# The FFN of a hybrid decoder block by 2x2 blocks in seven products

## The chip, the cores and the metric

The kernel runs on one core of a Trainium2 chip. A time is device microseconds of one execution; the kernel before takes 2752.7 us, the median of three runs (2752.18 to 2753.68).

## The reference

One decoder layer for 512 tokens of width 2048, in fp32: two attention branches, merged by sigmoid gates, and a SwiGLU FFN of width 5632. Only the FFN changes:

```python
    h2 = _rms(x, g_norm2) * (1 + sc2) + sh2
    gate, up = jnp.split(h2 @ w_ffn_in, 2, axis=-1)
    x = x + gt2 * ((jax.nn.silu(gate) * up) @ w_ffn_out)
```

`w_ffn_in` is 2048 x 11264, `w_ffn_out` 5632 x 2048; `sh2`, `sc2` and `gt2` are rows computed from the conditioning vector.

## The kernel before

An fp32 product is made of three matmuls. Each operand is kept as a high part (rounded to the matrix engine's fp32r) and a low part (the rest), and `mm3` sums high x low, high x high and low x high in PSUM. Activations lie with channels on the 128 partitions and tokens along the row (128x512). Weights are the standing operand, 128x128 at a time, and 512 tokens stream past: one output tile is 128 channels x 512 tokens.

The program is a list of steps. A step that needs weights gets a piece of 128x1024, cut from a load of 128x2048 that SP issues (`load`, four buffers). ScalarE copies the piece to `whi`, and VectorE subtracts to get `wlo` (three buffers each), before the step in front of it runs. VectorE, ScalarE and TensorE instructions are put in order by a scheduler where `Ordered` is off; with it on they keep program order.

The FFN's width is cut into 11 groups of four gate tiles and four up tiles. `last_a` and `last_b` make the last tile of the output projection in two token halves, so that the second norm of one half (`last_sum`, `last_row`, `norm2_half`) runs beside products. Group 0 runs k-tile by k-tile into eight PSUM banks (`ff0_first`, `ff0_second`, `ff0`), so each k-tile's norm (`norm_tile`) stands just ahead of its matmuls. Then `ff_in` makes each further group, 8 tiles x 16 k-tiles x 3 = 384 matmuls; `swiglu` evacuates a pair to `act`; and `ffn_out` makes the down projection of the group before, 16 tiles x 4 k-tiles x 3 = 192 matmuls, and VectorE adds each tile, times `gt2`, to the residual `x1`, which stays in SBUF. In the last group each finished tile is stored, 14 from POOL and 2 from SP.

Tiles of 128x512 come from one pool of 68. PSUM has eight banks under the names mm (3), s (2), t (2) and y (1). An instruction issued through `Ordered` has line 82 in every row; loads have line 173.

Of the kernel before, what the change touches and what calls it, by code (L numbers as in the profile page):

```python
# [1279 lines left out]
```

## Time and profile before

| | |
|---|---|
| median of three runs | 2752.7 us |
| span of the profiled execution | 2750.7 us |
| TensorE busy | 2710.9 us |
| VectorE busy | 1401.7 us |
| ScalarE busy | 838.7 us |
| mean DMA rate | 145 GB/s |

The profiled execution is one of the program's executions; its span runs from the first to the last instruction. Matmuls are pipelined, so their listed durations overlap. The time per matmul is the distance between starts.

### The profile page before, as it was taken

The page shows a single profiled execution, that of the slowest core. Times are in us where ns is not written, and L with a number is a line of the kernel's source. Part 1 is how long each engine was busy: PE and PEld are TensorE (multiplying, and loading weights), DVE is VectorE, ACT ScalarE, POOL GpSimd, SP SyncE. Part 2 cuts the span into 40 slices and gives each one's busy share as a digit, 9 for nine tenths or more (in the row PEclk, how much of TensorE's full clock was granted, in tenths as well). Part 3 has the DMA queues.
Part 4 walks back from the last instruction along what each step waited for, and adds up shares of the span by engine and source line. Part 5 has one row for each costly group of instructions (what it writes and reads, how often), then busy time and mean ns, then how long its engine had stood idle before and what let it go on. Part 6 is the DMA issues. An engine that isn't in the chain of part 4 may idle for free.

```text
span 2750.7 us, 30791 instructions
## 1 busy us (share of the span) xinstructions
PE 2710.9 (99%) x12760; PEld 2265.5 (82%) x12760; DVE 1401.7 (51%) x1870; ACT 838.7 (30%) x1145; POOL 39.3 (1%) x85
## 2 busy tenths in 40 slices
PE   5999999999999999999999999999999999999999
PEld 4788888888998888888888888888888888888887
DVE  8966766657887755433543424242424333333333
ACT  4334656533333322222322222222221222222221
POOL 0000000001001000000000000000000000000001
PEclk9999999999999999999999999999999999999999
DMA  9855444346666773332222222222222232232222
GB/s 345 291 189 172 161 137 136 134 158 245 245 232 255 287 297 130 134 122 93 99 101 92 97 102 92 95 105 92 93 106 92 93 107 92 92 107 92 92 105 79
DMA packets 69892, 398.04 MB, mean 145 GB/s; under 512 B 7861, under 2 KB 8117, under 8 KB 27769
## 3 DMA queue, kind: packets, MB, share of 16 engines
q1 hardware_dynamic: 62496, 381.45, 38.7%
q10 hardware_dynamic: 6056, 10.70, 1.0%
q0 software_dynamic: 1200, 3.93, 0.4%
q8 instruction: 100, 1.64, 0.2%
q14 instruction: 40, 0.32, 0.0%
HBM read 381.37 MB, written 14.68 MB: 144 GB/s over the span
## 4 chain that ended last, share of the span: by engine, by line
PE 96%; DVE 2%; DMA 1%; ACT 0%; issue 0%; SPq 0%; ACTq 0%; DVEq 0%
PE ps_mm L82 64%; PE ps_s L82 20%; PE ps_t L82 10%; PE ps_y L82 2%; DVE raw L266 1%; DVE wlo L82 0%; DMA raw<-in_w_ada_dram 0%; DMA xt<-in_xT_dram 0%; DMA gpark<-sg 0%; DVE hl L82 0%; DVE xt L82 0%; DMA consts<-in_consts_dram 0%; ACT whi L82 0%; DVE diag L82 0%; SPq L173 0%
## 5 line engine op out<-in xcount | busy, mean ns | idle before, releaser
L82 ACT CAST whi<-raw 128x1024 fp32r<-128x1024 f32 (+1 forms) x474 | 495.8, 1048 | 1479.9 <-PE ps_mm L82 812.9
L82 DVE TENSOR_TENSOR wlo<-raw,whi 128x1024 fp32r<-128x1024 f32 (+1 forms) x474 | 577.5, 1219 | 692.4 <-ACT whi L82 682.4
L82 PE MATMUL ps_mm<-h2l,whi 128*128 128x512 f32 (+1 forms) x1014 | 393.5, 388 | 0.0
L82 PE MATMUL ps_mm<-h2h,whi 128*128 128x512 f32 (+1 forms) x1014 | 393.2, 388 | 0.0
L82 PE MATMUL ps_mm<-h2h,wlo 128*128 128x512 f32 (+1 forms) x1014 | 393.2, 388 | 0.0
L82 PE MATMUL ps_mm<-hl,whi 128*128 128x512 f32 x832 | 327.5, 394 | 0.0
L82 PE MATMUL ps_mm<-hh,whi 128*128 128x512 f32 x832 | 325.4, 391 | 0.0
L82 PE MATMUL ps_mm<-hh,wlo 128*128 128x512 f32 x832 | 325.4, 391 | 0.0
L82 PE MATMUL ps_s<-acth,whi 128*128 128x512 f32 x704 | 273.9, 389 | 0.0
L82 PE MATMUL ps_s<-acth,wlo 128*128 128x512 f32 x704 | 273.9, 389 | 0.0
L82 PE MATMUL ps_s<-actl,whi 128*128 128x512 f32 x704 | 273.8, 389 | 0.0
L82 DVE SCALAR_TENSOR_TENSOR xr<-ps_s,ada_gt,xr 128x512 f32<-128x512 f32 x176 | 132.1, 751 | 230.9 <-PE ps_s L82 230.9
L266 DVE CUSTOM_DVE_ANT_0 raw<-raw,cb,cols 128x2048 f32<-128x2048 f32 x96 | 224.7, 2346 | 2.1 <-DMA raw<-in_w_ada_dram 2.1
L82 PEld LDWEIGHTS ps_mm<-h2l,whi 128*128 128x128 f32 x1014 | 190.4, 188 | 39.0
L82 PEld LDWEIGHTS ps_mm<-h2h,whi 128*128 128x128 f32 x1014 | 190.4, 188 | 39.0
L82 PEld LDWEIGHTS ps_mm<-h2h,wlo 128*128 128x128 f32 x1014 | 190.4, 188 | 39.0
L82 PEld LDWEIGHTS ps_mm<-hh,wlo 128*128 128x128 f32 x832 | 156.4, 188 | 32.4
L82 PEld LDWEIGHTS ps_mm<-hh,whi 128*128 128x128 f32 x832 | 156.7, 188 | 30.7
L82 PEld LDWEIGHTS ps_mm<-hl,whi 128*128 128x128 f32 x832 | 156.8, 188 | 30.5
L82 PEld LDWEIGHTS ps_s<-actl,whi 128*128 128x128 f32 x704 | 132.2, 188 | 27.6 <-DVE actl L82 0.3
L82 PEld LDWEIGHTS ps_s<-acth,wlo 128*128 128x128 f32 x704 | 132.2, 188 | 27.4
L82 PEld LDWEIGHTS ps_s<-acth,whi 128*128 128x128 f32 x704 | 132.2, 188 | 27.3
(283 smaller groups left out, 3671.6 us busy)
## 6 DMA issues: line engine op xcount, KB each, us to landing
raw<-in_w_ff_dram SPq DMA_DIRECT2D x132, 1024.0 KB, 4.7
raw<-in_w_ada_dram SPq DMA_DIRECT2D x96, 1024.0 KB, 5.2
raw<-in_w_gate_dram SPq DMA_DIRECT2D x27, 1024.0 KB, 5.0
raw<-in_w_sb_dram SPq DMA_DIRECT2D x24, 1024.0 KB, 4.9
raw<-in_w_out_dram SPq DMA_DIRECT2D x16, 1024.0 KB, 4.8
raw<-in_w_gate_dram SPq DMA_DIRECT2D x24, 512.0 KB, 4.5
raw<-in_w_lat_dram SPq DMA_DIRECT2D x8, 1024.0 KB, 8.2
gpark<-sg ACTq DMA_DIRECT2D x32, 256.0 KB, 5.2
```

Source lines behind the costliest of these rows:

```text
L82: ins = f(*a, **kw)
L266: tc.keep_in_program_order(nc.vector.tensor_tensor_reduce(raw, raw, cb, 1.0, col(C_B + 16 * ADA[name] + j), ALU.mult, ALU.add, dst))
```

## The change

The FFN's three matrices are cut into 2x2 blocks: tokens in halves of 256, the summed dimension in halves, the output columns in halves. Seven block products (P1, P5, P7, P3, P6, P2, P4, in this order) and sums of blocks give what eight products gave. Some products have a sum of activation blocks (x12, x34 and so on) on one side and a difference of weight blocks on the other.

- The roles are exchanged: a 128x128 block of activations stands and 512 weight columns stream past, so an output tile has 128 tokens x 512 channels. Gated activations are turned back on TensorE (`act_back1`, `act_back2`, 16 transposes a group).
- Weight blocks are 128x1024 in a pool of ten (`rp2`), loaded six pieces ahead. `piece_make` makes the difference of two raw blocks in place on VectorE where a product has one, then `whi` and `wlo`, two pieces ahead.
- Gate and up of all 11 groups come first, 7 products x 4 pieces x 12 = 336 matmuls a group. The activations' parts and sums are stored to DRAM (`apark`, 14 stores a group, from POOL). The down projection follows in five chunks of groups (`CH`), two column halves each, with 7 x 2 x 12 = 168 matmuls a group; the parts come back by loads from SP, and bank sums are added in `acc`.
- The second norm of all k-tiles is done by `first_norms`, before P1 of group 0, and `second_norms`, before the last piece of P1, which also makes the sums. The residual `x1` is written over by it and waits in DRAM (`xpark`, 17 stores from POOL). `out_tiles` turns the final sums back (64 transposes), loads the residual and stores the result.

```diff
+        ep_cm.__exit__(None, None, None)
+        rp_cm.__exit__(None, None, None)
+        st["rp2"] = ctx.enter_context(tc.tile_pool(name="rp2", bufs=10, reuse_waits="tile"))
+        ffn_begin()
         vec.on = act.on = pe.on = True
         last_mm(0, range(8, 16))
         last_evac(0)
...
+    def norm2(k, th):
         c = half_cols(th)
-        if th == 0:
-            h2.append((t2("h2h", F32R), t2("h2l", F32R)))
-        hi, lo = h2[k]
         gs, sh = ada["gs2"][:, k:k + 1], ada["sh2"][:, k:k + 1]
-        t = t2("nt")
-        vec.scalar_tensor_tensor(t[:, 0:256], x1[k][:, c], gs, st["rstd2"][:, c], ALU.mult, ALU.mult)
-        act.activation(hi[:, c], t[:, 0:256], AF.Identity, bias=sh)
-        vec.scalar_tensor_tensor(lo[:, c], t[:, 0:256], sh, hi[:, c].bitcast(F32), ALU.add, ALU.subtract)
+        t = x1[k][:, c]
+        vec.scalar_tensor_tensor(t, t, gs, st["rstd2"][:, c], ALU.mult, ALU.mult)
...
+    def sums(a, b, put):
+        lo, hi = slice(0, 256), slice(256, 512)
+        s12, s34 = t2("s12"), t2("s34")
+        vec.tensor_tensor(s12[:, lo], a[:, hi], b[:, hi], ALU.add)
+        vec.tensor_tensor(s12[:, hi], s12[:, lo], a[:, lo], ALU.subtract)
+        put(1, split_t(s12, "x12"))
+        vec.tensor_tensor(s34[:, lo], a[:, lo], a[:, hi], ALU.subtract)
+        vec.tensor_tensor(s34[:, hi], b[:, lo], s12[:, hi], ALU.subtract)
+        put(3, split_t(s34, "x34"))
...
+        sums(x1[j], x1[j + 8], put)
...
+    PROD = {
+        "P1": ((1, 1), "11", None), "P5": (1, "12", "11"), "P7": (3, "22", "12"), "P3": (4, "22", None),
+        "P6": (2, "22", "11"), "P2": ((1, 2), "21", None), "P4": ((2, 2), "21", "22"),
+    }
...
+    def piece_make(stage, g, prod, j):
+        _, x, y = PROD[prod]
+        key = (stage, g, x, j)
+        if y:
+            kd = (stage, g, INTO[prod], j)
+            vec.tensor_tensor(raws[kd], raws[key], raws[stage, g, y, j], ALU.subtract)
+            key = kd
+        r = raws[key]
+        hi = wp.tile([P, 1024], F32R, tag="whi", name=nm("whi"), bufs=3)
+        lo = wp.tile([P, 1024], F32R, tag="wlo", name=nm("wlo"), bufs=3)
+        v4 = lambda t: t.rearrange("p (k m c) -> p k m c", k=2, m=4)
+        act.copy(v4(hi), kmc(key, r))
+        vec.tensor_tensor(v4(lo), kmc(key, r), v4(hi).bitcast(F32), ALU.subtract)
+        for b in LAST.get(prod, ()):
+            del raws[stage, g, b, j]
+        return hi, lo
...
+    def ahead_to(i, n_make, n_load):
+        while cur["load"] < min(i + n_load + 1, len(pieces)) or cur["make"] < min(i + n_make + 1, len(pieces)):
+            if cur["load"] <= cur["make"] or cur["load"] < min(i + n_load + 1, len(pieces)):
+                for key in piece_keys(*pieces[cur["load"]]):
+                    raw_load(key)
+                cur["load"] += 1
+            else:
+                made[cur["make"]] = piece_make(*pieces[cur["make"]])
+                cur["make"] += 1
...
+                ahead_to(i, 2, 6)
...
+    def prod_mm(bank, hl, w, kk, first, last):
+        wh, wl = w
+        cs = slice(kk * 512, kk * 512 + 512)
+        xh, xl = hl
+        for t in range(2):
+            mm3(bank[t], (xh[:, t * P:(t + 1) * P], xl[:, t * P:(t + 1) * P]), (wh[:, cs], wl[:, cs]),
+                first, last, skip_group_check=True)
...
+        product("P1", "A", True, False)
+        copy_to("p1", "A")
+        if g > 0:
+            add_do(lambda: act_back2(g - 1))
+        product("P5", "B", True, False)
+        copy_to("z", "B")
+        product("P7", "C", True, False)
+        add_bank("z", "C")
+        product("P3", "B", False, True)
+        product("P6", "D", True, True)
+        def u_of(t):
+            vec.tensor_tensor(G["p1", t], G["p1", t], G["D"][t], ALU.add)
+            G["u", t] = G.pop(("p1", t))
+        both(u_of)
+        both(after_p6)
+        product("P2", "A", False, True)
+        both(after_p2)
+        product("P4", "C", False, True)
+        both(after_p4)
+        add_do(lambda: act_back1(g))
+        groups[g] = G
+    groups = {}
+    apark = [dp.tile([P, 7 * T], F32, name=f"apark_{i}") for i in range(2 * FG)]
...
+        def after_p6(t):
+            u, z = G["u", t], G["z", t]
+            vec.tensor_tensor(z, z, u, ALU.add)
+            c12 = t2("c12")
+            vec.tensor_tensor(c12, u, G["B"][t], ALU.add)
+            G["c12", t] = c12
...
+    def park(i, a, pair):
+        for part, t in enumerate(pair):
+            nc.gpsimd.dma_start(pk(i, a, 2, part), t.bitcast(F32).rearrange("p (a x) -> p a x", a=2))
...
+    def act_back1(g):
+        src = [groups[g].pop(("a1", t)) for t in range(2)]
+        for j in range(2):
+            o = ps(("mm", "y")[j])
+            back(src, j, o)
+            y = t2("y1")
+            act.copy(y, o)
+            park(2 * g + j, 0, split_t(y, "y1"))
+            yraw[g, j] = y
...
+    def act_back2(g):
+        src = [groups[g].pop(("a2", t)) for t in range(2)]
+        for j in range(2):
+            o = ps(("mm", "y")[j])
+            back(src, j, o)
+            y2 = t2("y2")
+            act.copy(y2, o)
+            y1 = yraw.pop((g, j))
+            x = t2("x22", F32R)
+            act.copy(x[:, 0:256], y2[:, 256:512])
+            vec.tensor_tensor(x[:, 256:512], y2[:, 256:512], x[:, 0:256].bitcast(F32), ALU.subtract)
+            nc.gpsimd.dma_start(apark[2 * g + j].rearrange("p (a x) -> p a x", x=T)[:, 2], x.bitcast(F32))
+            lo, hi = slice(0, 256), slice(256, 512)
+            s12, s34 = t2("s12"), t2("s34")
+            vec.tensor_tensor(s12[:, lo], y2[:, lo], y2[:, hi], ALU.add)
+            vec.tensor_tensor(s12[:, hi], s12[:, lo], y1[:, lo], ALU.subtract)
+            park(2 * g + j, 3, split_t(s12, "y12"))
+            vec.tensor_tensor(s34[:, lo], y1[:, lo], y2[:, lo], ALU.subtract)
+            vec.tensor_tensor(s34[:, hi], y1[:, hi], s12[:, hi], ALU.subtract)
+            park(2 * g + j, 5, split_t(s34, "y34"))
...
+    add_do(first_norms)
...
+    at_product(1, lambda: last_sum(1))
+    at_product(2, lambda: last_row(1))
+    def second_norms():
+        for k in range(8):
+            norm2(k + 8, 0)
+            norm2(k, 1)
+            norm2(k + 8, 1)
+            x_sums(k)
...
+    CH = ((0, 1, 2), (3, 4), (5, 6), (7, 8), (9, 10))
...
+                bank = B[BANK[prod]][t]
+                if ci == 0:
+                    a = t2("acc")
+                    act.copy(a, bank)
+                    acc[q, prod, t] = a
+                else:
+                    a = acc[q, prod, t]
+                    vec.tensor_tensor(a, a, bank, ALU.add)
+                if final:
...
+                add_piece(("b", (q, g), prod, 0), use)
+            add_do(lambda prod=prod: evac(prod))
+            if prod == "P1" and ci == q == 0:
+                add_do(lambda: act_back2(FG - 1))
+            if q == 1 and ci + 1 < len(CH):
+                add_do(lambda prod=prod: y_load(ci + 1, prod))
...
+    def out_tiles(q, col_):
+        xr_ = {}
+        for i in range(4):
+            m = 4 * (2 * q + col_) + i
+            xr = t2("xo")
+            sync_dma(xr, xpark[m])
+            xr_[i] = xr
+        for i in range(4):
+            m = 4 * (2 * q + col_) + i
+            o = ps(("mm", "y")[i % 2])
+            for r in range(2):
+                for t in range(2):
+                    pe.transpose(o[:, (2 * r + t) * P:(2 * r + t + 1) * P],
+                                 fin[q, r + 1, col_ + 1, t][:, i * P:(i + 1) * P], ident)
+            xr = xr_[i]
+            vec.scalar_tensor_tensor(xr, o, ada["gt2"][:, m:m + 1], xr, ALU.mult, ALU.add)
+            (nc.gpsimd if m < 14 else nc.sync).dma_start(outT[m * P:(m + 1) * P, :], xr)
```

The order of TensorE's work at the FFN's start. In `h2l` and `h2h` are the parts of one normed k-tile, in `x_...` and `x12...` those of a block and of a sum of two blocks. Before:

```order
L82 MATMUL ps_t_10680<-h2l_10647,whi_10564 128x256
L82 MATMUL ps_t_10680<-h2h_10646,whi_10564 128x256
L82 MATMUL ps_t_10680<-h2h_10646,wlo_10565 128x256
L82 MATMUL ps_t_10681<-h2l_10647,whi_10564 128x256
L82 MATMUL ps_t_10681<-h2h_10646,whi_10564 128x256
L82 MATMUL ps_t_10681<-h2h_10646,wlo_10565 128x256
L82 MATMUL ps_s_10682<-h2l_10647,whi_10564 128x256
L82 MATMUL ps_s_10682<-h2h_10646,whi_10564 128x256
```

Now, from the end of P1 into P5:

```order
L82 MATMUL ps_s_10794<-wlo_10828,x_10776 128x512
L82 MATMUL ps_s_10794<-whi_10827,x_10776 128x512 x2
L82 MATMUL ps_s_10795<-wlo_10828,x_10776 128x512
L82 MATMUL ps_s_10795<-whi_10827,x_10776 128x512 x2
L82 MATMUL ps_t_11103<-wlo_10850,x12h_10881 128x512
L82 MATMUL ps_t_11103<-whi_10849,x12h_10881 128x512
L82 MATMUL ps_t_11103<-whi_10849,x12l_10882 128x512
L82 MATMUL ps_t_11104<-wlo_10850,x12h_10881 128x512
L82 MATMUL ps_t_11104<-whi_10849,x12h_10881 128x512
L82 MATMUL ps_t_11104<-whi_10849,x12l_10882 128x512
```

The matmuls after P1 take the sum x12 where a single normed tile stood.

VectorE at the same place, before: norms of single tiles (`nt`, then `h2l`) beside `wlo`:

```order
L82 TENSOR_TENSOR wlo_10732<-raw_10729,whi_10731 128x1024
L82 SCALAR_TENSOR_TENSOR nt_10750<-xr_9557,ada_gs_160,rstd_10537 128x256
L82 SCALAR_TENSOR_TENSOR h2l_10647<-nt_10750,ada_sh_161,h2h_10646 128x256
L82 SCALAR_TENSOR_TENSOR nt_10754<-xr_9621,ada_gs_160,rstd_10537 128x256
L82 SCALAR_TENSOR_TENSOR nt_10820<-xr_9686,ada_gs_160,rstd_10537 128x512
L82 SCALAR_TENSOR_TENSOR h2l_10653<-nt_10754,ada_sh_161,h2h_10652 128x256
L82 SCALAR_TENSOR_TENSOR h2l_10823<-nt_10820,ada_sh_161,h2h_10822 128x512
```

Now (`xr` is normed in place, `s` holds a sum of blocks, `x12l` and `x34l` its low part):

```order
L82 SCALAR_TENSOR_TENSOR x_10873<-xr_10128,ada_sh_183,x_10873 128x256
L82 SCALAR_TENSOR_TENSOR xr_9732<-xr_9732,ada_gs_182,rstd_10596 128x256
L82 SCALAR_TENSOR_TENSOR xr_10260<-xr_10260,ada_gs_182,rstd_10596 128x256
L82 TENSOR_TENSOR s_1889_10877<-xr_9601,xr_10128 128x256
L82 SCALAR_TENSOR_TENSOR xr_9798<-xr_9798,ada_gs_182,rstd_10596 128x256
L82 TENSOR_TENSOR s_1889_10877<-s_1889_10877,xr_9601 128x256
L82 SCALAR_TENSOR_TENSOR xr_10326<-xr_10326,ada_gs_182,rstd_10596 128x256
L82 SCALAR_TENSOR_TENSOR xr_9864<-xr_9864,ada_gs_182,rstd_10596 128x256
L82 SCALAR_TENSOR_TENSOR xr_10392<-xr_10392,ada_gs_182,rstd_10596 128x256
L82 TENSOR_TENSOR x12l_10882<-s_1889_10877,x12h_10881 128x512
L82 TENSOR_TENSOR s_1890_10878<-xr_9601 128x256
L82 TENSOR_TENSOR s_1890_10878<-xr_10128,s_1889_10877 128x256
```

The norms of many tiles and the first sum stand between two `wlo`.

VectorE inside a group, before: `wlo` and the two operations of `swiglu`:

```order
L82 TENSOR_TENSOR silu_11841<-silu_11841,ps_mm_11786 128x512
L82 TENSOR_TENSOR wlo_11880<-raw_11877,whi_11879 128x1024
L82 TENSOR_TENSOR actl_11845<-silu_11841,acth_11844 128x512
L82 TENSOR_TENSOR wlo_11908<-raw_11877,whi_11907 128x1024
L82 TENSOR_TENSOR wlo_11939<-raw_11936,whi_11938 128x1024
L82 TENSOR_TENSOR wlo_11974<-raw_11936,whi_11973 128x1024
L82 TENSOR_TENSOR silu_11966<-silu_11966,ps_mm_11911 128x512
```

Now, at the end of P6 (`p`, `z`, `c` hold block sums, `raw<-raw,raw` is a difference of weight blocks):

```order
L82 TENSOR_TENSOR wlo_13225<-raw_2329_13149,whi_13224 128x1024
L82 TENSOR_TENSOR p_2278_12888<-p_2278_12888,ps_mm_13175 128x512
L82 TENSOR_TENSOR p_2279_12890<-p_2279_12890,ps_y_13176 128x512
L82 TENSOR_TENSOR z_13024<-z_13024,p_2278_12888 128x512
L82 TENSOR_TENSOR c_2344_13243<-p_2278_12888,ps_t_12957 128x512
L82 TENSOR_TENSOR z_13026<-z_13026,p_2279_12890 128x512
L82 TENSOR_TENSOR c_2345_13246<-p_2279_12890,ps_t_12958 128x512
L82 TENSOR_TENSOR wlo_13249<-raw_2332_13168,whi_13248 128x1024
L82 TENSOR_TENSOR wlo_13265<-raw_2337_13189,whi_13264 128x1024
L82 TENSOR_TENSOR raw_2329_13149<-raw_2329_13149,raw_2275_12869 128x1024
L82 TENSOR_TENSOR wlo_13284<-raw_2326_13130,whi_13283 128x1024
L82 TENSOR_TENSOR raw_2332_13168<-raw_2332_13168,raw_2298_12950 128x1024
```

Six operations of 512 columns now stand between one `wlo` and the next, and differences of weight blocks between those that follow.

## Rows read from the trace of the kernel before

**Rows 1.** page, busy time by engine, and the chain that ended last
```profile
PE 2710.9 (99%) x12760; PEld 2265.5 (82%) x12760; DVE 1401.7 (51%) x1870; ACT 838.7 (30%) x1145; POOL 39.3 (1%) x85
...
PE 96%; DVE 2%; DMA 1%; ACT 0%; issue 0%; SPq 0%; ACTq 0%; DVEq 0%
```

**Rows 2.** busy time by stretch: times, then PE, PEld, DVE, ACT, POOL, clock, DMA share, GB/s
```profile
15.00:20.00 5.00, 0.47 (x3) 0.47 (x3) 4.44 (x8) 4.44 (x8) 0.00 (x0) 1.00 1.04 399
985.00:1010.00 25.00, 25.00 (x112) 20.71 (x111) 14.94 (x18) 7.23 (x10) 0.00 (x0) 1.00 0.92 359
...
1500.00:2000.00 500.00, 500.00 (x2207) 414.20 (x2206) 180.16 (x186) 112.03 (x122) 0.00 (x0) 1.00 0.27 97
2700.00:2751.00 51.00, 46.97 (x207) 38.40 (x205) 20.66 (x24) 6.84 (x7) 7.58 (x14) 1.00 0.22 83
```

**Rows 3.** instructions in order of time, TensorE inside the FFN (start, duration)
```profile
1599.75 0.39 PE L82 MATMUL ps_mm<-h2h,whi 128*128 128x512 f32 x1
...
1602.92 0.39 PE L82 MATMUL ps_mm<-h2l,whi 128*128 128x512 f32 x1
```

**Rows 4.** the same view of TensorE, first FFN products and a gap
```profile
1305.57 0.39 PE L82 MATMUL ps_t<-h2l,whi 128*128 128x256 f32 x1
1305.79 0.28 PE L82 MATMUL ps_t<-h2h,whi 128*128 128x256 f32 x1
...
1308.33 0.61 PE L82 MATMUL ps_y<-ones,sq 128*128 128x1 f32 x4 [1.06 <-DVE sq L82]
```

**Rows 5.** chain of waits over the last 61 us (start, length)
```profile
2703.32 43.67 PE ps_s L82 x192
...
2747.01 0.75 DVE xr L82
```

**Rows 6.** groups by form, TensorE between 400 and 1000 us
```profile
L82 PE MATMUL ps_mm<-whi,hh 128*128 128x256 f32 x256 | 72.4, 283 | 0.0
...
L82 PE MATMUL ps_t<-consts,sa 128*128 128x128 f32 x80 | 11.3, 272 | 0.0
```

**Rows 7.** groups by form between 1450 and 2750 us, all engines
```profile
L82 DVE TENSOR_TENSOR wlo<-raw,whi 128x1024 fp32r<-128x1024 f32 x236 | 289.3, 1226 | 489.3 <-ACT whi L82 481.2
...
L82 ACT CAST whi<-raw 128x1024 fp32r<-128x1024 f32 x236 | 248.4, 1053 | 995.5 <-PE ps_mm L82 496.1 <-PE ps_s L82 336.9 <-PE ps_t L82 162.4
...
L82 DVE SCALAR_TENSOR_TENSOR xr<-ps_s,ada_gt,xr 128x512 f32<-128x512 f32 x162 | 121.6, 751 | 212.8 <-PE ps_s L82 212.8
...
L82 ACT CAST acth<-silu 128x512 fp32r<-128x512 f32 x40 | 24.5, 612 | 0.0
...
L1156 POOL DMA_DIRECT2D out_dram<-xr x14 | 7.6, 542 | 1819.2 <-DVE xr L82 1819.2
```

**Rows 8.** instructions in order of time, VectorE during the attention
```profile
380.56 0.69 DVE L82 CUSTOM_DVE_ANT_0 p<-ps_s,rstd 128x512 f32<-128x512 f32 x1
381.18 0.08 DVE L82 DVE_READ_ACCUMULATOR2_ANT mx<- 128x1 f32 x1
...
383.29 1.23 DVE L82 TENSOR_TENSOR wlo<-raw,whi 128x1024 fp32r<-128x1024 f32 x1
384.44 0.16 DVE L82 RECIPROCAL ri<-sm 128x1 f32<-128x1 f32 x1
...
385.09 0.42 DVE L82 TENSOR_TENSOR ptl<-ps_t,pth 128x256 fp32r<-128x256 f32 x1
```

**Rows 9.** the same view of VectorE, second norm of the first token half
```profile
1303.96 0.48 DVE L82 SCALAR_TENSOR_TENSOR nt<-xr,ada_gs,rstd 128x256 f32<-128x256 f32 x1 [1.26 <-ACT rstd L82]
1305.03 0.49 DVE L82 SCALAR_TENSOR_TENSOR h2l<-nt,ada_sh,h2h 128x256 fp32r<-128x256 f32 x1 [0.58 <-ACT h2h L82]
1305.43 0.48 DVE L82 SCALAR_TENSOR_TENSOR nt<-xr,ada_gs,rstd 128x256 f32<-128x256 f32 x1
```

**Rows 10.** DMA issues: count, KB each, median us from issue to landing
```profile
gpark<-sg ACTq DMA_DIRECT2D x32, 256.0 KB, 5.2
...
out_dram<-xr POOLq DMA_DIRECT2D x14, 256.0 KB, 2.3
```

More of the change, by code (lines that the diff above doesn't have):

```diff
@@ L129 @@
     ypark = [dp.tile([P, T], F32, name=f"ypark_{g}") for g in range(H)]
-    onesw = cp.tile([P, T], F32, name="onesw")
+    xpark = [dp.tile([P, T], F32, name=f"xpark_{g}") for g in range(KD)]
+    onesw = ep.tile([P, T], F32, name="onesw")
     nc.gpsimd.memset(onesw, 1.0)
@@ L175, in load @@
     def load(src, w=2048):
-        raw = wp.tile([P, w], F32, tag="raw", name=nm("raw"), bufs=4)
+        raw = rp.tile([P, w], F32, tag="raw", name=nm("raw"))
         sync_dma(raw, src)
@@ L239, in run_steps @@
             s[0](ahead.pop(i))
-    cb = cp.tile([P, D], F32, name="cb")
+    cb = ep.tile([P, D], F32, name="cb")
     cps = []
@@ new lines, with add_piece, add_do @@
+    ev = []
+    made = {}
+    cur = {"load": 0, "make": 0}
+    pieces = []
+    def add_piece(args, use):
+        pieces.append(args)
+        ev.append((len(pieces) - 1, use))
+    def add_do(fn):
+        ev.append((None, fn))
+    def ahead_to(i, n_make, n_load):
[7 more added lines that the diff above has]
+                cur["make"] += 1
@@ new lines, in tb, with ffn_in_group, product, use @@
+    def tb(*tags):
+        return [ps(t) for t in tags]
+    def ffn_in_group(g, order):
+        G = {}
+        n = KD // 4
+        def product(prod, bank, start, stop):
+            def use(w, j):
+                if j == 0 and start:
+                    G[bank] = tb(*{"A": ("s", "s"), "B": ("t", "t"), "C": ("mm", "mm"), "D": ("mm", "y")}[bank])
+                for kk in range(2):
+                    prod_mm(G[bank], X[PROD[prod][0], 2 * j + kk], w, kk, start and j == 0 and kk == 0,
+                            stop and j == n - 1 and kk == 1)
+            for j in range(n):
+                add_piece(("a", g, prod, j), lambda w, j=j: use(w, j))
+        def both(fn):
+            add_do(lambda: [fn(t) for t in range(2)])
+        def copy_to(name, bank):
+            def fn(t):
+                G[name, t] = t2(name)
+                act.copy(G[name, t], G[bank][t])
+            both(fn)
+        def add_bank(name, bank, out=None):
+            def fn(t):
+                dst = G[name, t] if out is None else t2(out)
+                vec.tensor_tensor(dst, G[name, t], G[bank][t], ALU.add)
+                G[out or name, t] = dst
+            both(fn)
+        def after_p6(t):
[4 more added lines that the diff above has]
+            G["c12", t] = c12
+        def after_p2(t):
+            s = t2("silu")
+            act.activation(s, G["A"][t], AF.Silu)
+            vec.tensor_tensor(s, s, G["c12", t], ALU.mult)
+            G["a1", t] = s
+            G["c12", t] = None
+        def after_p4(t):
+            u = G["u", t]
+            vec.tensor_tensor(u, u, G["C"][t], ALU.add)
+            act.activation(u, u, AF.Silu)
+            vec.tensor_tensor(u, u, G["z", t], ALU.mult)
+            G["a2", t] = u
+            G["z", t] = None
+        product("P1", "A", True, False)
[19 more added lines that the diff above has]
+        groups[g] = G
@@ L1183 @@
+    for ci in range(len(CH)):
+        for q in range(2):
+            ffn_out_chunk(ci, q)
+            if ci == len(CH) - 1:
+                for col_ in (1, 0):
+                    add_do(lambda q=q, col_=col_: out_tiles(q, col_))
     run_steps()
+    run_ev()
 def _km(w):
```

208 lines of the change are left out of this document (130 added, 78 removed).

## The prediction

> **What bounds the kernel now.** The page's first part comes first: TensorE is busy 2710.9 of 2750.7 us, VectorE 51%, ScalarE 30%, and the chain that ended last is 96% TensorE [rows 1]. So the question is what TensorE issues in the stage that changes, and who could make it wait there. The busy time by stretch says that the FFN stage is steady: TensorE fills 500.00 of 500.00 us between 1500 and 2000 with 2207 matmuls, which is 500 / 2207 = 0.2266 us each, at a granted clock of 1.00, while VectorE works 180 us of it and the DMA share is 0.27 [rows 2]. The instructions in order of time show the same step: matmuls of 512 columns start 0.22 to 0.23 us apart though each is listed with 0.39 us, since they are pipelined [rows 3]. The step is the price, not the duration.
>
> The FFN's first matmul starts at 1305.57 [rows 4], the last ends at 2747.0 [rows 5]. That is 1441.4 us. FFN products are 11 x (384 + 192) = 6336 matmuls, so 6336 x 0.2266 = 1435.7 us are issue, and 5.7 us are gaps, at the start of the stage, where TensorE stands before the second norm [rows 4].
>
> **Matmuls.** Seven products of half size in each dimension take the place of eight: per group 7 x 4 x 12 = 336 for gate and up and 7 x 2 x 12 = 168 for down, with the same 512 columns and three matmuls for the two parts. All groups: 11 x 504 = 5544, which is 792 fewer. Whether the weights stream and the activations stand or the reverse: with 256 columns both kinds are in the trace, a moving whi at 283 ns [rows 6] and a standing one at 0.28 us [rows 4], so I keep 0.2266. 5544 x 0.2266 = 1256.3 us, a saving of 179.5.
>
> **Transposes.** The gated activations now have tokens on the partitions and are turned back, 16 transposes per group, and the result by 64 at the end: 240. In the trace 80 such of 128 columns took 11.3 us, 0.141 each [rows 6]. All stand on TensorE: 240 x 0.141 = 33.8 us.
>
> **VectorE beside the products.** Before, a 128x1024 subtraction of raw and whi served 24 matmuls. Now one serves 12, and four of seven products first subtract two raw blocks, so a piece with both has 2.3 to 2.5 us of VectorE for 2.72 us of matmuls (12 x 0.2266). A group has 28 wlo, 16 differences, 20 operations of 512 and 10 of 256 columns. By the mean durations (1.226, 0.69 and 0.42 us [rows 7, 8]; an operation with a PSUM operand and one without differ little) that is 54.0 + 13.8 + 4.2 = 72 us. By the spacing of consecutive starts, which is what a queue of ready instructions takes (1.15 for 1024 columns, 0.62 for 512 [rows 8], 0.40 for 256 [rows 9]), it is 67. TensorE has 336 x 0.2266 + 16 x 0.141 = 78.4 us per group. VectorE would go from 36% busy in this stage to 85 to 92%, and stays under. But whi and wlo have three buffers and are made two pieces ahead, 5.4 us, and six operations of 512 (3.9 us) come at once after P6. I followed the listed order by hand with these spacings: VectorE stays just ahead, and TensorE waits 0.5 to 1.5 us a group, at P5 and P7, where the sums of the turned-back activations fall in, and at P2. I take 1 us, 11 in all. Bounds: nothing, and 4 us a group (44 in all), if the six operations and their handoffs lie bare. ScalarE, with 28 whi of 1.05 and some 20 copies and activations of 0.6 us [rows 7], 42 us per group, hides.
>
> In the down projection a pair of groups has 28 x 1.15 + 16 x 1.15 + 28 evacuations x 0.63 = 68 us for 76.1 us of matmuls; the first chunk evacuates on ScalarE. I take 1 us a chunk, 5 in all, with bounds 0 and 20.
>
> **Start of the FFN.** Here something is late that was not. Before, the norm of one k-tile ran just ahead of its matmuls. P5 needs x12, which adds two quarters of the normed residual, so the norm of all k-tiles and all token halves must come first, and TensorE has only P1 and P5 meanwhile (2 x 4 x 12 matmuls, 21.8 us from 1305.6). After the last residual half, at about 1308, VectorE has: 72 operations of 256 x 0.40 = 28.8; 16 of 512 x 0.62 = 9.9; 14 of 1024 x 1.15 = 16.1; small ones of the norm about 2: 56.8 us. It is done no earlier than 1365. Handoffs to ScalarE and back (nt 1303.96, h2l 1305.03: 1.07 us a round, where the two VectorE operations alone are 0.8 [rows 9]) add some 5 to 10: 1370 to 1375. P5's last two k-tiles need the last x12, so P5 ends at about 1376, where without waits it would end at 1327.4. The stall is 48 us. Bounds: 30, if the sums go first and the x34 half of the work slides under P7, and 70, if each of eight rounds waits on ScalarE for 3 us more.
>
> A stall like this has a second price in the Trainium skill (TensorE: Matmul & The Clock Gate, "HAM oscillation — how this bites in real kernels"): an engine left idle between bursts loses its full clock and starts the next burst at half. The row that bears on it speaks against: between 15 and 20 us TensorE was busy 0.47 of 5 us and the granted clock was 1.00 [rows 2]. By the rule the last 12 matmuls of P5 and the first 12 of P7 would each take 0.2266 us longer behind the stall, 5.4 us, and the time would be 2680; by the row it stays 2675, and I go by the row.
>
> **Transfers.** 154 stores of 256 KB park the parts (40 MB) and as many loads bring them back. The weights come in rows of 1 KB instead of 8 KB. The heaviest half chunk asks for 0.6 MB of weights and 1 MB of the next chunk's parts per product of 24 matmuls, 5.44 us: 295 GB/s. The trace had 359 GB/s at a share of 0.92 in 985:1010 [rows 2], so I cost them at nothing; without that cover, at 250 GB/s say, four half chunks of 38 us would each be 18% longer, 27 us. The 17 stores of the residual cost POOL 0.54 us each [rows 7] beside products.
>
> **End.** In the last chunk the results are added, turned and joined to the residual. At the end of the first column half TensorE waits for about 8.5 us of VectorE work (two evacuations, two additions, transposes between eight joins of 0.75 us [rows 7]), less what the transposes fill: 4 us. After the last product: two evacuations and two additions (2.5 us), eight joins (6.0), then the issue of 0.54 us and the landing of 2.3 us of a store [rows 7, 10], and about 2 for residual tiles that SP loads late, behind stores that wait for VectorE: 13.5 us, of which 4.5 are the 32 transposes already counted, so 9 more. Before, 3.7 us lay behind the last matmul.
>
> **Sum.** 1305.6 + 1256.3 + 33.8 + 48 + 11 + 5 + 4 + 9 = 2672.7 us of span. The profiled execution had a span of 2750.7 and the median of the runs is 2752.7, so 2 us lie around it: 2675 us, 2.8% less. A check: a group of gate and up should go from 87.0 us (384 matmuls) to about 79.4, one of down from 43.5 to about 38.5.
>
> **Rival A: the handoffs lie bare.** There are 11 x 7 + 5 x 2 x 7 = 147 product ends. The forecast leaves 77 us below the time before, so from 0.53 us of further wait at each, the change gains nothing. For it: VectorE at 85 to 92%, in order, with only two pieces ahead, and a wlo behind a burst delays all that follow. At 0.8 us each the time is 2675 + 118 = 2793. Against it: TensorE never waits for a wlo between 1500 and 2000 [rows 2], and ScalarE has half its time free. If waits of 0.3 us are the case, 2719.
>
> **Rival B: parking holds the buffers.** The activation parts take 56 of the 68 tiles of 128x512, and 12 rotate. Their stores go out on POOL at 0.54 us issue [rows 7] and land 2.3 us later when idle, 5.2 us for stores amid traffic [rows 10]. If the tiles for y12 and y34 wait for landings of 5 us, VectorE loses 3 to 5 us a group, and it has only 6 to 11 to spare: 11 x 4 = 44 us, 2719. A rule of the Trainium skill speaks for this (SBUF — State Buffer, "SBUF: two separate sides"): stores issued from POOL wait when VectorE holds the port they share. The same page infers that tensor_tensor does not hold what descriptors need. No row here shows such stores under a busy VectorE: those at the end came with VectorE 41% busy [rows 2]. If each of the 14 stores a group waited out one operation of 1.2 us, POOL would have 14 x 1.7 = 24 us of each 78, so it keeps up, and only the landings matter.
>
> **Rival C: the start goes well.** If the scheduler lets x12 of all tiles go ahead of x34, 30 us of stall, and no handoff waits: 2641.
>
> **Rival D: the seven products do not shrink the stage**, because a moving matmul of 512 columns with a standing operand of 128 costs more than 0.2266. 0.014 us (6%) more each takes the gain back, 5544 x 0.014 = 78; at 10% the time is 2675 + 126 = 2801. The 256-wide rows agree [rows 4, 6], so this has little chance.
>
> **How the numbers follow.** Two times differ here if they are 0.2% (5.5 us) apart; closer is no change. Forecast, 2655 to 2700: 0.52. B and mild A (0.2 to 0.4 us a product), 2700 to 2747: 0.20. C, under 2655: 0.10. Strong A, slower: 0.14. D: 0.01. In between, within 0.2%: 0.03. So faster 0.82, same 0.03, slower 0.15. The range from 2635 (C with a little less at the end) to 2755 leaves out about 0.04 below and 0.13 above.
>
> **What would show it.** TensorE's matmul count by 512 columns falls by 792 and steps stay 0.2266. One gap of 40 to 55 us around 1320 to 1375, with VectorE full and the clock at 1.00. Group periods 79 to 80 us, waits of TensorE for wlo at P5, P7 and P2. VectorE 85 to 92% busy from 1400 on. A tail of 13 us. The forecast is wrong if a group takes over 84 us (A or B: the releaser is then a 512 operation of VectorE, or a store), or if the start gap is outside 30 to 70.

## The result and the profile after

The changed kernel takes 2692.3 us, the median of four runs (2691.28 to 2694.34), against 2752.9 before (the three runs named at the top and a fourth): a ratio of 0.978, 95% interval 0.9766 to 0.9794. The forecast was 2675 in a range of 2635 to 2755. The profiled execution has a span of 2689.6 us, 17 us more than the forecast's 2672.7.

The page's first part answers to [rows 1]: VectorE goes from 51% to 75% of the span, and TensorE from 99% to 96%, so it now waits somewhere. The row of TensorE's granted clock, in tenths over 40 slices, was all 9 before, shown first here, and is no longer.

```profile
PEclk9999999999999999999999999999999999999999
```

```profile
PE 2584.3 (96%) x12166; PEld 2147.2 (80%) x12166; DVE 2024.8 (75%) x2614; ACT 1149.4 (43%) x1557; POOL 154.9 (6%) x256
...
PEclk9999999999999999999879999999999999999998
```

Busy time by stretch (the columns are those of [rows 2]) shows where. The two lower slices in the middle are the FFN's start: TensorE is busy 21.65 of 50 us in 1330:1380, at a mean granted clock of 0.53, mostly the lower of its two levels (1.2 and 2.4 GHz), and VectorE is not full either. The last slice is the end, where TensorE stands before the final joins. Inside gate and up TensorE lacks 1.1 us in 80. The down projection is full in the row shown.

```profile
1310.00:1330.00 20.00, 13.04 (x45) 9.92 (x44) 19.60 (x49) 12.94 (x28) 0.00 (x0) 0.83 0.00 0
1330.00:1380.00 50.00, 21.65 (x45) 13.24 (x46) 37.89 (x68) 24.41 (x45) 0.00 (x0) 0.53 0.07 21
1640.00:1720.00 80.00, 78.90 (x356) 64.99 (x355) 67.33 (x75) 39.73 (x48) 9.66 (x14) 1.00 0.48 153
2300.00:2400.00 100.00, 100.00 (x443) 82.81 (x442) 78.77 (x75) 46.50 (x51) 0.00 (x0) 1.00 0.61 194
```

TensorE in order of time answers to [rows 3]: the first of these matmuls to the last is 14 steps in 3.17 us, 0.2264 each, with the weights streaming.

```profile
1479.05 0.39 PE L82 MATMUL ps_t<-wlo,x34h 128*128 128x512 f32 x1
...
1482.22 0.39 PE L82 MATMUL ps_mm<-whi,x12l 128*128 128x512 f32 x1
```

And four transposes take 0.43 or 0.44 us, 0.109 each, where [rows 6] had 0.141:

```profile
1446.35 0.60 PE L82 MATMUL ps_mm<-consts,p 128*128 128x128 f32 x4
1446.79 0.60 PE L82 MATMUL ps_y<-consts,p 128*128 128x128 f32 x4
...
1468.04 0.50 PE L82 MATMUL ps_mm<-wlo,x34h 128*128 128x512 f32 x1 [1.52 <-DVE wlo L82]
```

The last of these rows is the one wait that each group from the second on has, for a wlo, in P7: 1.52 us here, 1.1 in most groups. The view of waits lists what TensorE waited for after the start: 15 waits for a wlo, ten of them these, 5.7 us the longest (where the down projection begins), and five for the joins at the end of the two column halves.

```profile
PE ps_mm L82 <- DVE wlo L82: 19.0, 15, 5.7
PE ps_y L82 <- DVE xo L82: 8.6, 5, 3.8
```

The forecast's terms beside the trace, by the stretches between rows that can be found in it:

| stretch | forecast, us | trace, us |
|---|---|---|
| up to the first FFN matmul (1306.31) | 1305.6 | 1306.3 |
| to the end of P5 of group 0 (1379.10) | 69.8 | 72.8 |
| to the end of group 10's products (2230.36) | 849.3 | 851.3 |
| to the last chunk's first half (2622.29) | 388.0 | 391.9 |
| its output tiles (to 2629.99) | 8.5 | 7.7 |
| the last half's products (to 2670.00) | 38.1 | 40.0 |
| to the end of the span | 13.5 | 19.6 |
| sum | 2672.8 | 2689.6 |

Both kinds of cost hide in the third row: the transposes were 0.032 us cheaper than forecast, 160 x 0.032 = 5.1 us, and the waits dearer.

### The profile page after: what moved, and what is told of

The parts are those of the page before. It is cut to its first block, busy times and chain, and to the rows that moved or that the text cites. A ratio compares the mean times of both kernels' runs of the same rounds, so it can differ in the third digit from the quotient of the medians.

```text
span 2689.6 us, 32101 instructions
## 1 busy us (share of the span) xinstructions
PE 2584.3 (96%) x12166; PEld 2147.2 (80%) x12166; DVE 2024.8 (75%) x2614; ACT 1149.4 (43%) x1557; POOL 154.9 (6%) x256
## 4 chain that ended last, share of the span: by engine, by line
PE 71%; issue 17%; DVE 6%; DMA 3%; ACT 2%; POOL 0%; SPq 0%; POOLq 0%; ACTq 0%; DVEq 0%
PE ps_mm L82 48%; PE ps_s L82 11%; PE ps_t L82 8%; PE ps_y L82 5%; DMA raw<-in_w_ff_dram 2%; DVE wlo L82 2%; DVE raw L271 1%; ACT whi L82 1%; DVE s L82 0%; DVE raw L82 0%; DMA gpark<-sg 0%; DMA raw<-in_w_ada_dram 0%; POOL out_dram L1487 0%; DVE x L82 0%; DVE xr L82 0%
## 5 line engine op out<-in xcount | busy, mean ns | idle before, releaser
L82 ACT CAST whi<-raw 128x1024 fp32r<-128x1024 f32 x672 | 702.8, 1050 | 1037.7 <-PE ps_mm L82 471.6
L82 DVE TENSOR_TENSOR wlo<-raw,whi 128x1024 fp32r<-128x1024 f32 x672 | 815.7, 1218 | 341.2 <-ACT whi L82 338.5
L82 DVE TENSOR_TENSOR raw<-raw,raw 128x1024 f32<-128x1024 f32 x264 | 319.2, 1220 | 20.9 <-DMA raw<-in_w_ff_dram 17.7
L82 PE MATMUL ps_s<-whi,x 128*128 128x512 f32 x704 | 218.6, 392 | 0.1
L82 PEld LDWEIGHTS ps_s<-whi,x 128*128 128x128 f32 x704 | 133.3, 189 | 28.1 <-DVE x L82 0.6
L82 PE MATMUL ps_s<-wlo,x 128*128 128x512 f32 x352 | 139.3, 396 | 1.8 <-ACT x L82 1.8
L82 PE MATMUL ps_mm<-whi,yb 128*128 128x512 f32 x440 | 137.0, 393 | 0.0
L82 PE MATMUL ps_s<-whi,yb 128*128 128x512 f32 x352 | 108.5, 389 | 0.0
L82 PE MATMUL ps_t<-whi,yb 128*128 128x512 f32 x352 | 108.5, 389 | 0.0
L82 PE MATMUL ps_mm<-whi,x 128*128 128x512 f32 x352 | 108.4, 389 | 0.0
```

What stands on the lines that cost most here:

```text
L82: ins = f(*a, **kw)
```

## The experiments

Each was made from the changed kernel (2692.3 us) unless it says otherwise.

**The start: order of norms and sums.** The stall from 1327 to 1379 could be VectorE's work or its waits for ScalarE. The norms of k-tile k + 2 and the additions of k + 1 are emitted ahead of the splits of k.

```diff
-            norm2(k + 8, 0)
-            norm2(k, 1)
-            norm2(k + 8, 1)
-            x_sums(k)
...
+            if k + 2 < 8:
+                norms(k + 2)
+            if k + 1 < 8:
+                adds(k + 1)
+            splits(k)
```

> The norms and sums at the start of the FFN are emitted two k-tiles apart, so that no VectorE instruction stands right behind the ScalarE instruction that it needs. Theory (the stall is VectorE waiting on ScalarE, 6 to 8 us a k-tile in turn): P5 of group 0 ends at 1366 to 1372 instead of 1379, time 2680 to 2686. Rival (the stall is the amount of VectorE work, or the loads behind the raw blocks): P5 ends within 3 us of 1379, time 2689 to 2695.

2677.6 us (2675.91 to 2679.18), ratio 0.9727 (0.9712 to 0.9741): 14.7 us less than the changed kernel. VectorE of the changed kernel, in order of time over one k-tile (in brackets what it waited for before):

```profile
1359.08 0.87 DVE L82 SCALAR_TENSOR_TENSOR x<-xr,ada_sh,x 128x256 fp32r<-128x256 f32 x2
1360.53 0.43 DVE L82 TENSOR_TENSOR s<-xr,xr 128x256 f32<-128x256 f32 x1 [0.58 <-ACT xr L82]
1360.99 0.42 DVE L82 TENSOR_TENSOR s<-s,xr 128x256 f32<-128x256 f32 x1
1362.10 0.69 DVE L82 TENSOR_TENSOR x12l<-s,x12h 128x512 fp32r<-128x512 f32 x1 [0.68 <-ACT x12h L82]
1362.71 0.42 DVE L82 TENSOR_TENSOR s<-xr 128x256 f32<-128x256 f32 x1
1363.05 0.42 DVE L82 TENSOR_TENSOR s<-xr,s 128x256 f32<-128x256 f32 x1
1364.15 0.69 DVE L82 TENSOR_TENSOR x34l<-s,x34h 128x512 fp32r<-128x512 f32 x1 [0.69 <-ACT x34h L82]
1366.16 1.23 DVE L82 TENSOR_TENSOR wlo<-raw,whi 128x1024 fp32r<-128x1024 f32 x1 [1.32 <-ACT whi L82]
```

It waits for ScalarE four times: three times in the 5.8 us from the first row to the end of x34l, and once more for a whi. With the edit:

```profile
1338.89 0.87 DVE L82 SCALAR_TENSOR_TENSOR x<-xr,ada_sh,x 128x256 fp32r<-128x256 f32 x2
1339.68 0.42 DVE L82 TENSOR_TENSOR s<-xr,xr 128x256 f32<-128x256 f32 x1
1340.02 0.42 DVE L82 TENSOR_TENSOR s<-xr 128x256 f32<-128x256 f32 x1
1340.35 0.42 DVE L82 TENSOR_TENSOR s<-s,xr 128x256 f32<-128x256 f32 x1
1340.69 0.48 DVE L82 SCALAR_TENSOR_TENSOR xr<-xr,ada_gs,rstd 128x256 f32<-128x256 f32 x1
1341.08 0.42 DVE L82 TENSOR_TENSOR s<-xr,s 128x256 f32<-128x256 f32 x1
1341.42 0.68 DVE L82 TENSOR_TENSOR x12l<-s,x12h 128x512 fp32r<-128x512 f32 x1
1342.02 0.48 DVE L82 SCALAR_TENSOR_TENSOR xr<-xr,ada_gs,rstd 128x256 f32<-128x256 f32 x1
1342.41 0.68 DVE L82 TENSOR_TENSOR x34l<-s,x34h 128x512 fp32r<-128x512 f32 x1
```

No waits, and 4.1 us for a k-tile, with two norms in it. P5 ends at 1362.80, 16 us earlier; this and the time are below what was expected. Some of it comes back later: the third product then waits 1.3 us for its weights. By stretch, from the last residual half to P5's end, the changed kernel first:

```profile
1308.00:1379.10 71.10, 35.79 (x98) 24.17 (x97) 59.48 (x119) 38.69 (x76) 0.00 (x0) 0.63 0.05 15
```

```profile
1308.00:1362.80 54.80, 32.92 (x100) 22.81 (x99) 54.80 (x118) 38.92 (x80) 0.00 (x0) 0.71 0.00 0
```

VectorE stood idle for 11.6 of 71.1 us, by the view of waits for ScalarE, and with the edit not at all; the other 5 us are work that now comes behind P5's end. So the waits that the theory names are real, and they were 11.6 us of the stall's 51. The greater part was VectorE's work: with the edit it is full throughout, and 34 us of stall are left.

**The start: the clock.** Products that nothing reads fill TensorE's gaps in P5 of group 0.

```diff
+                    if g == 0 and prod == "P5":
+                        dummies(28)
                     prod_mm(G[bank], X[PROD[prod][0], 2 * j + kk], w, kk, ...
...
-    at_product(2, lambda: last_row(1))
+    at_product(2, lambda: (dummies(16), last_row(1)))
```

> Between the bursts of P5 in group 0, and before the second norm's row, TensorE runs products of 256 columns that nothing reads (28 before each k-tile, 16 before the row). Theory (the granted clock fell to 0.50 because TensorE stood idle, and the slow bursts lie on the chain, since the next whi waits for them): the clock stays at 1.00 through 1320 to 1380, six matmuls take 1.4 us instead of 2.9, and P5 ends 3 to 6 us sooner, time 2686 to 2690. Rival (the bursts are beside the chain): the clock stays up and P5 ends at 1379 or later, time 2691 to 2698. Third: the clock falls all the same, and the extra products cost up to 30 us.

2687.6 us (2686.78 to 2689.89), ratio 0.9765 (0.9749 to 0.9782): 4.7 us less. TensorE in P5 of the changed kernel, and by stretch the same time with the edit:

```profile
1362.12 0.79 PE L82 MATMUL ps_t<-wlo,x12h 128*128 128x512 f32 x1 [3.23 <-ACT x12h L82]
1362.71 0.63 PE L82 MATMUL ps_t<-whi,x12h 128*128 128x512 f32 x1
...
1364.42 0.63 PE L82 MATMUL ps_t<-whi,x12l 128*128 128x512 f32 x1
```

```profile
1330.00:1380.00 50.00, 40.93 (x246) 35.52 (x245) 38.76 (x66) 27.62 (x50) 0.00 (x0) 0.93 0.08 22
```

```profile
1354.88 0.50 PE L82 MATMUL ps_t<-wlo,x12h 128*128 128x512 f32 x1 [1.95 <-ACT x12h L82]
1355.22 0.40 PE L82 MATMUL ps_t<-whi,x12h 128*128 128x512 f32 x1
...
1356.41 0.40 PE L82 MATMUL ps_t<-whi,x12l 128*128 128x512 f32 x1
```

A matmul's step goes from 0.43 to 0.23 us, the mean granted clock over 1330:1380 from 0.53 to 0.93, and P5 ends at 1376.12 instead of 1379.10. So the slow bursts lay on the chain: in the changed kernel three whi (at 1350.71, 1365.09 and 1379.34) each waited 0.97 us for TensorE to be done with an older one, and with the edit the last two of these waits are gone. The clock's fall cost 3 us up to P5's end and 4.7 in all.

**Ten raw weight blocks.** What makes the wait of 1.1 to 1.5 us in each P7? The first attempt took the two halves of `act_back2` side by side, to spare VectorE four waits for ScalarE (the edit is put in words):

```diff
         for j in range(2):
-            (transposes, x22, s12, y12, s34, y34 of half j)
+            (transposes of half j)
+        (s12 of both halves, y12 of both, s34 of both, y34 of both, x22 of both)
```

> In each group the two halves of the second turned-back activations are taken side by side instead of one after the other. Theory (the 1.1 us wait of TensorE in each group is a wlo queued behind VectorE's four waits of 0.7 us on ScalarE there): the wait falls under 0.4 us in each of ten groups and by some 3 us where the down projection starts, time 2680 to 2685. Rival (VectorE's load as such, 84% busy, makes the wait): it stays 1.1 us, time 2690 to 2694.

2703.6 us (2701.87 to 2708.11), ratio 0.9824 (0.9809 to 0.9838): 11.3 us more, against both theories. VectorE's order of time shows a candidate in both kernels: the difference of weight blocks for P7 waits for a load. The changed kernel first, then the edit.

```profile
1459.83 1.22 DVE L82 TENSOR_TENSOR raw<-raw,raw 128x1024 f32<-128x1024 f32 x1 [1.21 <-DMA raw<-in_w_ff_dram]
...
1464.38 1.23 DVE L82 TENSOR_TENSOR raw<-raw,raw 128x1024 f32<-128x1024 f32 x1 [0.31 <-DMA raw<-in_w_ff_dram]
```

```profile
1462.19 1.23 DVE L82 TENSOR_TENSOR raw<-raw,raw 128x1024 f32<-128x1024 f32 x1 [2.18 <-DMA raw<-in_w_ff_dram]
...
1466.21 1.23 DVE L82 TENSOR_TENSOR raw<-raw,raw 128x1024 f32<-128x1024 f32 x1 [0.45 <-DMA raw<-in_w_ff_dram]
```

The wait for the load is 1.21 us and becomes 2.18. SP issues a load when one of the ten raw blocks comes free, and a load takes 5.4 us to land (the median). By the code, a weight block of the 2x2 comes in four raw blocks, and when P7 begins the four of `11` (needed until P6) and the four of `12` are still held. So of ten raw blocks two are left for the four of `22` that P7 subtracts from. So the number of blocks was changed next, to 11 (with 67 tiles of 128x512 in place of 68, to make room) and to 9.

```diff
-    tp = ctx.enter_context(tc.tile_pool(name="tp", bufs=68))
+    tp = ctx.enter_context(tc.tile_pool(name="tp", bufs=67))
...
-        ... tc.tile_pool(name="rp2", bufs=10, reuse_waits="tile")
+        ... tc.tile_pool(name="rp2", bufs=11, reuse_waits="tile")
```

> Eleven raw weight blocks instead of ten (and 67 tiles of 128x512 instead of 68, to make room). Theory (the 1.1 us wait of a group is the third product's weights: their load is issued only when a block comes free, and VectorE's difference waits for its landing): the wait falls to under 0.5 us a group, time 2682 to 2688. Rival (VectorE's own queue makes the wait): 1.0 to 1.2 us a group as before, time 2691 to 2694.

2672.8 us (2671.9 to 2673.58), ratio 0.9709 (0.9693 to 0.9725): 19.5 us less, beyond the expectation, which counted 1.1 us a group. A group takes 79.58 us in the changed kernel, 1.7 more than its matmuls and transposes, and 11 x 1.7 = 19 us. With eleven blocks it takes 77.98 (ten in 779.8 us). TensorE's waits for a wlo are 5 where they were 15: those in P7 are gone.

```profile
PE ps_mm L82 <- DVE wlo L82: 7.3, 5, 5.7
```

> Nine raw weight blocks instead of ten. Theory (loads wait for blocks): TensorE's waits grow by 2 to 5 us a group in gate and up, time 2715 to 2750. Rival (VectorE's queue): 2691 to 2698.

2819.8 us (2818.17 to 2821.32), ratio 1.0243 (1.0223 to 1.0264): slower than the kernel before the change, and far above what either theory said. The same 400 us of gate and up, by stretch, with 9, 10 and 11 blocks:

```profile
1400.00:1800.00 400.00, 363.90 (x1546) 294.98 (x1545) 294.04 (x321) 172.84 (x207) 38.67 (x56) 0.95 0.41 131
```

```profile
1400.00:1800.00 400.00, 393.97 (x1771) 324.61 (x1770) 335.91 (x371) 199.67 (x242) 48.38 (x70) 1.00 0.48 152
```

```profile
1400.00:1800.00 400.00, 400.00 (x1806) 332.04 (x1805) 341.29 (x375) 202.97 (x245) 48.37 (x70) 1.00 0.48 152
```

With 11, TensorE fills the stretch; with 10 it lacks 6.0 us, with 9 it lacks 36 and the clock falls to 0.95. By the view of waits VectorE's differences wait for loads 12.1, 17.7 and 95.7 us in all between 1400 and 2230:

```profile
DVE raw L82 <- DMA raw<-in_w_ff_dram: 12.1, 10, 1.7
```

```profile
DVE raw L82 <- DMA raw<-in_w_ff_dram: 17.7, 19, 1.4
```

```profile
DVE raw L82 <- DMA raw<-in_w_ff_dram: 95.7, 36, 4.5
```

With eleven, VectorE still waits 1.2 us for a load once a group, but early enough that TensorE does not. So TensorE's wait was the late loads', and one block is worth 19.5 us on one side and 127 on the other. The tile less that goes with the eleventh block was not tried alone.

**Rival A: how far ahead the parts are made.**

```diff
-                ahead_to(i, 2, 6)
+                ahead_to(i, 1, 6)
```

> The weight parts are made one piece ahead instead of two. If the handoffs lie nearly bare (rival A of the prediction), VectorE's bursts of six operations now meet TensorE directly: 2 to 4 us a product with a burst, some 4 to 10 us a group and 2740 to 2810. If the buffers, not the order of the program, set how far ahead the parts are made: 2690 to 2705.

2691.4 us (2691.13 to 2691.72), ratio 0.9777 (0.9757 to 0.9797): no difference. This agrees with the second reading, that the scheduler puts the instructions in order by itself and the three buffers, which stay, set how far ahead the parts are made. The edit was therefore a weak test of the handoffs. The stronger one is the stretch above: with 11 blocks TensorE is full, at a VectorE load of 341 in 400 us (85%). In gate and up the handoffs do not lie bare.

**Rival B: parking.** Each store of a part is made twice, to two places.

```diff
-            nc.gpsimd.dma_start(pk(i, a, 2, part), ...)
+            for which in (apark, apark2):
+                nc.gpsimd.dma_start(pk(which[i], a, 2, part), ...)
...
```

> Each parked part of the activations is stored twice, to two places in DRAM, 28 stores a group from POOL instead of 14, and a tile comes free only when both have landed. If parking holds the buffers (rival B of the prediction), TensorE loses 2 to 6 us more a group: 2715 to 2760. If the stores are hidden: 2690 to 2700.

2723.3 us (2722.49 to 2724.17), ratio 0.9893 (0.9873 to 0.9913): 31 us more. That is what rival B asks for, but its cause can be another: VectorE's waits for weight loads grow from 17.7 to 42.4 us, and it has none for a store.

```profile
DVE raw L82 <- DMA raw<-in_w_ff_dram: 42.4, 24, 3.6
```

So the doubled stores were run with 11 raw blocks (and one tile of 128x512 less).

> The doubled stores together with eleven raw weight blocks (67 tiles). Theory (the doubled stores cost through late weight loads, for which ten blocks leave no slack): with one block more most of the 31 us goes, time 2673 to 2690. Rival (the stores hold the tiles of 128x512, of which there is now one less): 2700 to 2730.

2683.7 us (2683.64 to 2683.74), ratio 0.975 (0.9731 to 0.977). Of the 31 us, 11 are left over the kernel with 11 blocks and single stores. So most of the cost went through late weight loads: between 1400 and 2200 their median landing went from 5.8 us to 6.4 with the doubled stores. What is left can be the tiles after all: here ScalarE's copy `z` of P5's sums waits nine times, 11.9 us in all, for a parked store to land, which it does nowhere in the kernel with 11 blocks and single stores. No run tests that. Single stores, as the change has them, were not taken away in any run, so what they cost is not known.

**The end.** All eight residual tiles of a column half are loaded before its first store.

In words in brackets, how many each call loads:

```diff
-            sync_dma(xr, xpark[m])          (four, for each of two calls)
+            sync_dma(xr, xpark[4 * (2 * q + c) + i])   (eight, in the first call)
```

> The residual tiles of a column half are all loaded ahead of the first store of the end. Theory (the last four loads stand on SP behind two stores that wait for VectorE): TensorE's last gap of 3.8 us goes, time 2687 to 2689. Rival (the landing of the last store sets the end whatever comes before): 2691 to 2694.

2688.6 us (2687.44 to 2690.73), ratio 0.9767 (0.9753 to 0.9782): 3.7 us less. VectorE's last joins of the changed kernel had waited for these loads:

```profile
2678.73 0.75 DVE L82 SCALAR_TENSOR_TENSOR xo<-ps_mm,ada_gt,xo 128x512 f32<-128x512 f32 x1 [3.82 <-DMA xo<-xpark]
2679.97 0.75 DVE L82 SCALAR_TENSOR_TENSOR xo<-ps_y,ada_gt,xo 128x512 f32<-128x512 f32 x1 [0.49 <-DMA xo<-xpark]
...
2681.93 0.75 DVE L82 SCALAR_TENSOR_TENSOR xo<-ps_y,ada_gt,xo 128x512 f32<-128x512 f32 x1 [0.54 <-PE ps_y L82]
```

With the edit these two waits are gone, and its last join starts at 2679.36.

**Together.** Order of the start, loads at the end, and 11 blocks:

> Three of the edits together: norms and sums at the start two k-tiles apart, residual loads ahead at the end, eleven raw blocks. If the three places are apart in time and each stands on TensorE's path, the gains add: 2692.3 - 14.7 - 3.7 - 19.5 = 2654 (2650 to 2659). If two of them remove the same wait: 2660 to 2673.

2655.0 us (2654.32 to 2655.67), ratio 0.9646 (0.9632 to 0.966). The three gains add within 1 us. This is the fastest kernel of the study, 97.6 us below the one before the change.

With the halves of `act_back2` side by side too:

> The kernel before this one in the list, and the two halves of the second turned-back activations side by side. Theory (taken alone that edit lost 11 us since it met late weight loads, which the eleventh block ends): it now gains by the gap where the down projection starts, 2 to 6 us, time 2648 to 2653. Rival (the edit itself costs VectorE or TensorE time): 2660 to 2668.

2664.8 us (2662.0 to 2667.69), ratio 0.9682 (0.9667 to 0.9696): 9.8 us more, so the eleventh block does not end that edit's loss, and my theory for it fell. The gap where the down projection begins did shrink (PE in 2200:2300: 94.28 us without, 97.05 with), but in 1380:1800 TensorE falls from 420.00 to 416.30. What in the new order costs this was not settled by a run. The trace has a candidate: ScalarE's copy `z` takes a tile whose parked store has not landed, in nine groups, and the `whi` copies of the next pieces stand behind it. With the old order (b1) there is no such wait.

```profile
ACT z L82 <- DMA apark<-y34h: 28.5, 9, 4.0
```

That is rival B's mechanism, in another kernel than the one it was named for. VectorE's waits for loads are longer too (16.4 us where b1 has 12.4, between 1432 and 2200).

And P2 of group 0 right behind P1, its weights loaded once more. The edit also splits the second norms: `norm2(k + 8, 0)` of all k-tiles stays before P1's last piece, the other norms and the sums come one piece later:

```diff
         copy_to("p1", "A")
+        if g == 0:
+            product("P2", "A", False, True)
...
-    at_product(3, second_norms)
+    at_product(3, lambda: [norm2(k + 8, 0) for k in range(8)])
+    at_product(4, second_norms)
```

> The kernel before this one in the list, and in group 0 the product P2, which needs no sum, right behind P1 (its weights are loaded a second time for P4). Theory (the start is a wait of TensorE for VectorE's norms and sums, and 10.9 us of products fit into it): 5 to 10 us less, 2640 to 2647. Rival (P2's four wlo delay the norms as much as P2 saves): within 3 us of the one before.

2657.1 us (2655.7 to 2658.0), ratio 0.9652 (0.9636 to 0.9668): 7.7 us below the kernel that it was added to. The gain is what the theory said (by the end of group 0 the traces are 5.2 us apart), though P2's move and that of the norms are not separated; the number expected was missed because the kernel that it was added to came out 12 us above its own expectation. It was not run with b1's order of `act_back2`.

## Why the prediction was right, and where it was off

**Matmul count and step.** Right. The step with streaming weights is 0.2264 us, and rival D (a dearer step) is out.

**Transposes.** 0.109 us and not 0.141, 240 x 0.032 = 7.7 us too much in the sum. The row of before was a mean over transposes of another stage. It was luck that this error hid part of the others: with 0.109 the forecast of the span is 2665.0, and the miss 25 us instead of 17.

**Start.** 48 us of stall forecast. The trace has 72.8 us from the first matmul to P5's end for 21.8 of work: 51. The size held, and so did its main parts: I put 57 us on VectorE's work, which was busy 59.5 from 1308 to P5's end, and 5 to 10 on handoffs, which were 11.6. What I had wrong is the order: e_skew takes 16 us out of P5's end by order alone, so this stall was not the least that the work allows. VectorE was not full, though I said that it would be. And I went by the row of 15:20, where the clock stayed at 1.00 with TensorE idle. Here it fell to 0.50, after waits of 4.5 and 5.9 us between bursts, and cost 4.7 us (e_warm). What the Trainium skill states (TensorE: Matmul & The Clock Gate, "HAM oscillation — how this bites in real kernels"), that an engine idle between bursts starts the next one slow, agrees with this trace. That the 5.4 us worked out by it come near is in part luck: I had 24 slow matmuls behind one stall, and the trace has 42 and more in bursts, most of whose cost lay beside VectorE's work. Why the row at 15:20 shows 1.00 stays open.

**Gate and up.** 1 us of wait a group was forecast; with 10 groups in 795.78 us (1434.58 to 2230.36) a group takes 79.58, against 79.4. Less 76.1 of matmuls and 1.7 of transposes that is 1.7. The size was nearly right, within its bounds, and P7 was one of the three places named; P5 and P2 have no wait. The reason given, sums of the turned-back activations that fall in there, is not what ends the wait: it is a weight load that waits for a raw block. I cost the transfers at nothing, from their rate. The rate was not the limit in this stage (a DMA share of 0.48); the number of blocks was, and the loss with 9 blocks shows that the sign of the forecast hung on it. None of the four rivals had this.

**Down projection.** 5 us spread over the chunks was forecast. By the table it is 431.9 us against 426.1, some 11 us more than its matmuls and transposes. The trace has one gap of 5.7 us where it begins, where VectorE is in the last `act_back2` and its handoffs; behind the gap the next matmuls run at a lower clock (a mean of 0.93 granted over 2250:2300); from 2300 on the stretches are full up to the last chunk, which has four waits for a wlo, 1.6 us in all.

**End.** 13.5 us forecast (its parts add to 13.3), 19.6 measured. The late residual loads were in the sum with 2 us and cost 3.7 (e_tail). The other part is behind the last join: VectorE's last one starts at 2681.93, ends at 2682.68, and the span ends 6.9 us later, where I had 2.8 for a store. The stores of the output land 2.3 to 3.0 us after their issue, so the landing fills less than half of it. The last store is now POOL's, and was SP's. Whether that is the reason was not tried.

**Rivals.** A (bare handoffs): out for gate and up, by TensorE's full stretch at 85% of VectorE. B (parking): in the changed kernel the tiles are not what is waited for, with a single wait of 0.2 us for a parked store between 1400 and 2230; doubled stores delay weights, and in b2 and with doubled stores and 11 blocks the tiles are waited for too. The page on SBUF (the Trainium skill, SBUF — State Buffer, "SBUF: two separate sides") has POOL's stores wait while VectorE runs an operation in a two-port mode. In this trace the parked stores landed in 2.6 to 4.5 us (medians by tile) with VectorE 84% busy, against 2.3 us for the stores of [rows 10]. That is at most 2.2 us more, under more DMA traffic, and which of the two causes it no run separates. C (a start of 30 us): not as built, but the order of e_skew, with 34, comes near it.

## What to carry to other kernels

When weights pass through a ring of blocks and an operation needs two of them at once, count the blocks that are alive at the tightest product and the time from a block's release to the next landing: one block more or less was worth 20 and 127 us here, with DMA half idle. A producer chain that crosses two engines for every tile should be emitted with the tiles staggered, so that neither engine stands behind the other: it ended 11.6 us of waits here. An idle gap on TensorE was paid twice here, since the next burst ran at a lower clock (4.7 us at the start).

## What was not expected of the hardware

- TensorE's granted clock was 0.50 to 0.51, the lower of its two levels, while it was busy 2.67, 0.49 and 3.16 of three times 5 us, in 1330 to 1345. Before, it was 1.00 with 0.47 of 5 us, near the program's start [rows 2].

```profile
1330.00:1335.00 5.00, 2.67 (x6) 1.66 (x6) 5.00 (x10) 2.38 (x6) 0.00 (x0) 0.51 0.00 0
1335.00:1340.00 5.00, 0.49 (x2) 0.00 (x0) 5.00 (x8) 3.28 (x6) 0.00 (x0) 0.50 0.00 0
1340.00:1345.00 5.00, 3.16 (x6) 1.66 (x6) 5.00 (x9) 2.04 (x4) 0.00 (x0) 0.50 0.00 0
```

- The same clock applies to transposes: four took 0.44 us in full clock, and 0.91 (2627.26 to 2628.17) behind a gap at the end of the first column half, at a granted clock of 0.58 in 2627:2628 and 0.50 in 2628:2629.
